# Raw weight panels in a ring of six after the mixers, with the constants' space given back

## The chip, the cores and the metric

The kernel runs on one core of one Trainium2 chip, as one launch. The metric is device time in microseconds (us) for the whole launch; a run's figure is that of the core, and the kernel's figure is the median of its runs. Traces are from the hardware profiler, one execution each.

## The reference

One decoder layer over 256 tokens of width 2048, in float32. A projection feeds two mixers (a causal multi-window pool and an RWKV-7 time mix); their outputs are concatenated and projected back; then a squared-ReLU channel mixer with 8192 hidden units, a gated per-layer embedding, and a final norm.

```python
h = rms_norm(x, attn_norm[i])
z = h @ w_in[0]
...                                      # token shift, pool mixer, RWKV-7 scan
mix = jnp.concatenate([pool_out, rwkv_out], axis=-1).astype(x.dtype)
x = x + mix @ w_out[i]

h2 = rms_norm(x, mlp_norm[i])
x = x + jnp.square(jax.nn.relu(h2 @ w_ffn_up[i])) @ w_ffn_down[i]

gate = jax.nn.sigmoid(rms_norm(x, ple_norm[i]) @ w_ple_gate[i])
x = x + gate * (p[i] @ w_ple_proj[i])
return rms_norm(x, final_norm)
```

## The kernel before

**Weights as panels.** All large weights stream from HBM once, in panels of 128 partitions x 1024 float32 (512 KB). `load_raw` (L146) takes a slot of the tag `raw` of the pool `wp`, which has three buffers, and issues one DMA from SyncE (its queue is SPq in the profile; the DMA is L148). A float32 panel is then split in two rounded parts, a high one by ScalarE (`wh`, two copies of 512 columns) and the remainder by VectorE (`wl`, one subtraction over 1024 columns). `wh` and `wl` are rings of three too. TensorE forms each product as three matmuls (high x high, low x high, high x low). The helper is `split_w` (L151; its instructions are L157 and L158); in the down projection it is `halves_of` (L1228, L1229).

**Stages.** The mixers run first, interleaved with the input projection and with half of the output projection by a hand-written order; TensorE's order is the program's up to `order.close()`. From there on a scheduler orders all engines at build time, by priority (splits and some evictions are raised by `high_priority`) and by its own model of when data and slots come free. The order on each engine, SyncE's DMA queue included, is then fixed: an instruction that waits holds up those behind it on its engine.

After that point:

- the second half of the output projection, `w_out`, 16 panels (`raw_o`), followed by the transposes `h2t`;
- `ffn_half(0)`: 64 panels of `w_ffn_up` (`raw_u`, `gemm_wide`, L1102 and L1107), then two down sweeps of 32 panels of `w_ffn_down` each (`raw_d`, `down_sweep`, L1217 to L1219), one for each half of the output columns;
- `ffn_half(1)`: the same again;
- the embedding's projection (4 panels, `raw_pp`), the gate (24 panels, `raw_gt`) and the end.

**A down sweep** goes through 16 steps `kp` of two panels (`rx`, `ry`). Most steps have 24 matmuls and two splits, `wh_d_7a`/`wl_d_7a` and `wh_d_7b`/`wl_d_7b` for step 7. The steps 1, 3, 6, 8, 11, 13 (`SEVEN`; in the last sweep 1, 3, 6, 11) take seven products for eight, 21 matmuls, at the price of four additions of panel quarters on VectorE (`td`, L1257 to L1260) and four splits: `wad` (L162, L163) and those named b, c and d. The d halves sit in the two buffers of the tag `graw`.

**Panels kept for the end.** In the last sweep (before steps 5, 8, 11, 14) and in the gate stage, `keep` (L1159 to L1164) loads a panel of the last gate quarter through the same two `graw` buffers and splits it into `gk`. Its DMA goes out on the same SyncE queue, and its split on the same ScalarE and VectorE queues.

**Memory.** `const` is a pool that lives to the end, and holds also what only the mixers read (`sbd`, `wband`, `zf`, `hsel`, `cmask` and others). `rctx` is the stack of pools that live through the mixers alone (`psr`, `rp`). It is closed behind the mixers, and the pool `fp`, for the feed-forward part, is opened in the space of `rp`.

Of the kernel before, what the change touches and what calls it, by code (L numbers as in the profile page):

```python
# [9 lines left out]
F32 = mybir.dt.float32  # L10
F32R = mybir.dt.float32r
# [5 lines left out]
T = 256  # L17
# [23 lines left out]
def trunk(  # L41
# [21 lines left out]
    const = ctx.enter_context(tc.tile_pool(name="const", bufs=1))  # L63
    wp = ctx.enter_context(tc.tile_pool(name="wp", bufs=3))
    act = ctx.enter_context(tc.tile_pool(name="act", bufs=1))
    psm = ctx.enter_context(tc.tile_pool(name="psm", bufs=4, space=PSUM))
    rctx = ctx.enter_context(ExitStack())
    psr = rctx.enter_context(tc.tile_pool(name="psr", bufs=4, space=PSUM))

    def mm_bank(name):  # L70
# [13 lines left out]
    def col(name, j):  # L84
        o = PARAM_COLS[name] + j
        return par_sb[:, o : o + 1]
# [6 lines left out]
    nc.vector.memset(eps_g, GN_EPS)  # L93
    ident = const.tile([128, 128], F32, name="ident")
    make_identity(nc, ident)
    ones = const.tile([128, 128], F32, name="ones")
    nc.vector.memset(ones, 1.0)
    jsum = const.tile([128, 128], F32, name="jsum")
    cmask = const.tile([128, 128], F32, name="cmask")
    rmask = const.tile([128, T], F32, name="rmask")  # L100
    sbd = [const.tile([128, 4, 128], F32, name=f"sbd{i}") for i in range(2)]
    nc.gpsimd.memset(cmask, 0.0)
    for r0 in (0, 64):
        nc.gpsimd.memset(cmask[r0 : r0 + 64, r0 : r0 + 64], 1.0)
    nc.gpsimd.tensor_copy(jsum, cmask)
    cen = const.tile([128, 128], F32, name="cen")
    jhead = const.tile([128, 32], F32, name="jhead")
    nc.gpsimd.memset(jhead, 0.0)
    nc.gpsimd.tensor_copy(jhead[:, 0:2], cmask[:, ::64])
    for r0 in (0, 64):  # L110
# [3 lines left out]
    nc.gpsimd.memset(rmask.rearrange("p (c t) -> p c t", t=64)[:, :, 0:1], 0.0)  # L114
    for i in range(2):
        nc.vector.memset(sbd[i], 0.0)
    edge = const.tile([128, 4, 16], F32, name="edge")
    nc.vector.memset(edge, 1.0)
    for g, win in enumerate(WINDOWS):
        for t in range(win - 1):  # L120
            nc.gpsimd.memset(edge[:, g, t : t + 1], float(win) / (t + 1))


    wband = const.tile([128, 4, 272], F32, name="wband")

    def make_bands():
        for g, win in enumerate(WINDOWS):
# [6 lines left out]
            nc.vector.tensor_tensor(w0[:, 0:128], w0[:, 0:128], ident, op=ALU.subtract)  # L134

    m0, m1 = PARAM_COLS["mu_r"], PARAM_COLS["mu_wag"] + 3
    omu = const.tile([128, m1 - m0], F32, name="omu")
    oka = const.tile([128, 8], F32, name="oka")

    def derived():  # L140
        ka0 = PARAM_COLS["k_a"]
# [1 line left out]
        nc.vector.tensor_scalar(oka, par_sb[:, ka0 : ka0 + 8], -1.0, 1.0, op0=ALU.mult, op1=ALU.add)  # L143
        nc.vector.scalar_tensor_tensor(cen, jsum, -1.0 / 64.0, ident, op0=ALU.mult, op1=ALU.add)

    def load_raw(src, n, name):  # L146
        raw = wp.tile([128, 1024], F32, tag="raw", name=f"raw_{name}")
        nc.sync.dma_start(raw[:, 0:n], src)  # L148
        return raw

# [32 lines left out]
    def gemm_cols(src, acts, name, consume, hooks=()):  # L183

        banks = [mm_bank(f"{name}_b{i}") for i in range(2)]
        nkp = src.shape[0]
        hooks = dict(hooks)
        for kp in range(nkp):
            if kp in hooks:
                hooks[kp]()  # L190
            raw = load_raw(src[kp].rearrange("p a n -> p (a n)"), 1024, f"{name}_{kp}")
            halves = split_w(raw, f"{name}_{kp}")
            for part in range(2):
                for a in range(2):
                    k = kp * 2 + a
                    ah, al = acts(k)
                    for ct in range(4):
                        o = banks[ct // 2][:, (ct % 2) * T : (ct % 2 + 1) * T]
                        w_ = halves[a][part][:, ct * 128 : (ct + 1) * 128]
                        if part:  # L200
                            nc.tensor.matmul(o, w_, ah, start=False, stop=k == 2 * nkp - 1, skip_group_check=True)
                            yield 0.12
                        else:
                            nc.tensor.matmul(o, w_, ah, start=k == 0 and ct % 2 == 0, stop=False, skip_group_check=True)
                            nc.tensor.matmul(o, w_, al, start=False, stop=False, skip_group_check=True)
                            yield 0.24
        consume(banks)

    def gemm_toks(src, acts, name, consume, kps=None, hooks=()):

        banks = [mm_bank(f"{name}_b{i}") for i in range(2)]
        kps = list(range(src.shape[0])) if kps is None else kps
        hooks = dict(hooks)
        for i, kp in enumerate(kps):
            if kp in hooks:
                hooks[kp]()
            raw = load_raw(src[kp].rearrange("p a n -> p (a n)"), 1024, f"{name}_{kp}")
            halves = split_w(raw, f"{name}_{kp}")
            for part in range(2):
                for a in range(2):  # L220
                    k = kp * 2 + a
                    a_ = acts(k)
                    ah, al = a_ if isinstance(a_, tuple) else (a_[:, 0, :], a_[:, 1, :])
                    for tt in range(2):
                        ts_ = slice(tt * 128, (tt + 1) * 128)
                        if part:
                            last = i == len(kps) - 1 and a == 1
                            nc.tensor.matmul(banks[tt], ah[:, ts_], halves[a][1], start=False, stop=last)  # L228
                            yield 0.23
                        else:  # L230
                            nc.tensor.matmul(banks[tt], ah[:, ts_], halves[a][0], start=i + a == 0, stop=False)  # L231
                            nc.tensor.matmul(banks[tt], al[:, ts_], halves[a][0], start=False, stop=False)  # L232
                            yield 0.45
        consume(banks)
# [40 lines left out]
    def run(gen):  # L275
        for _ in gen:
            pass
# [36 lines left out]
    nc.gpsimd.memset(hsel_f, 1.0)  # L314
    nc.gpsimd.affine_select(hsel_f, hsel_f, [[2048, 4], [1, 128]], ALU.is_ge, 0.0, base=0, channel_multiplier=-64)
    nc.gpsimd.affine_select(hsel_f, hsel_f, [[-2048, 4], [-1, 128]], ALU.is_ge, 0.0, base=63, channel_multiplier=64)
    hsel = const.tile([128, 4, 128], F32R, name="hsel")
    nc.gpsimd.tensor_copy(hsel, hsel_f)

    def flat(t_):  # L320
# [119 lines left out]
        nc.scalar.activation(rs1, sbank[:, 0:2], AF.Sqrt, bias=eps_n, scale=1.0 / D)  # L440
        nc.vector.reciprocal(rs1, rs1)

    zf = const.tile([128, 3, T], F32, name="zf")
    zwa, zg, zg2 = zf[:, 0], zf[:, 1], zf[0:64, 2]

    def wag_out():
# [518 lines left out]
    def pool_weights(i):  # L965
        praw = load_raw(pool_w[i].rearrange("p w k n -> p (w k n)"), 1024, f"pw{i}")
        t_ = rp.tile([128, 2, 2, 512], F32R, tag="AR", bufs=2, name=f"pws{i}")
        for wi in range(2):
            split_sb(t_[:, wi, 0], t_[:, wi, 1], praw[:, wi * 512 : (wi + 1) * 512])
        return [(t_[:, wi, 0], t_[:, wi, 1]) for wi in range(2)]  # L970
# [86 lines left out]
    def residual(banks, n):  # L1057
        for tt in range(2):
            xs = xr[tt][:, n * 512 : (n + 1) * 512]
            with tc.high_priority(30000):  # L1060
                nc.vector.tensor_tensor(xs, banks[tt], xs, op=ALU.add)
# [20 lines left out]
    fp = ctx.enter_context(tc.tile_pool(name="fp", bufs=1))  # L1082
    psw = ctx.enter_context(tc.tile_pool(name="psw", bufs=2, space=PSUM))

    def wide_bank(name):
        return psw.tile([128, 2, 512], F32, tag="wide", name=name)
# [25 lines left out]
    def transposed(name):  # L1112

        hl = fp.tile([128, 2, NK, T], F32R, tag="h2", name=name)
        h, l = hl[:, 0], hl[:, 1]

        def part(norm, n):
            for j2 in range(2 * n, 2 * n + 2):
                if j2 % 2 == 0:
                    b = wide_bank(f"{name}t")  # L1120
                for jj in range(2):
                    j = 2 * j2 + jj
                    for tt in range(2):
                        nc.tensor.transpose(
                            b[:, j2 % 2, jj * T + tt * 128 : jj * T + (tt + 1) * 128], xr[tt][:, j * 128 : (j + 1) * 128], ident
                        )
                for jj in range(2):
                    j = 2 * j2 + jj
                    src = b[:, j2 % 2, jj * T : (jj + 1) * T]
                    nc.scalar.activation(h[:, j, :], src, AF.Copy, scale=col(norm, j))  # L1130
                    nc.vector.scalar_tensor_tensor(
                        l[:, j, :], src, col(norm, j), h[:, j, :].bitcast(F32), op0=ALU.mult, op1=ALU.subtract
                    )

        return part, lambda k: hl[:, :, k, :]

    h2_part, h2 = transposed("h2")
    for n in range(4):
        run(gemm_toks(w_out[n], mix, f"o{n}", lambda banks: residual(banks, n), (6, 7, 2, 3)))
        h2_part("mlp_norm", n)  # L1140
# [331 lines left out]
```

## Time and profile before

| what | value |
|---|---|
| runs | 1190.15, 1193.17, 1196.21 us; median 1193.17 |
| profiled execution | 1191.21 us, its span 1189.5 us, granted clock 0.998 |
| TensorE matmul, weight load | 1169.6 us (98%), 974.0 us (82%) |
| VectorE, ScalarE, GpSimd | 859.2 us (72%), 702.5 us (59%), 14.0 us (1%) |
| DMA | 216.81 MB, mean 182 GB/s |

The stages after the mixers, by the busy time of the engines in them (windows chosen by hand; PE is the matmul row, DVE is VectorE, ACT is ScalarE):

| stage | window, us | PE | DVE | ACT | DMA share |
|---|---|---|---|---|---|
| output projection | 332 to 377 | 45.00 of 45 | 27.96 | 21.98 | 0.56 |
| up, first half | 377 to 556 | 178.44 of 179 | 118.12 | 97.58 | 0.58 |
| sweep 1 | 556 to 642 | 85.30 of 86 | 71.08 | 47.96 | 0.61 |
| sweep 2 | 642 to 729 | 85.89 of 87 | 73.60 | 48.31 | 0.62 |
| up, second half | 729 to 905 | 176.00 of 176 | 117.36 | 91.41 | 0.59 |
| sweep 3 | 905 to 989 | 84.00 of 84 | 70.73 | 47.73 | 0.61 |
| sweep 4 | 989 to 1080 | 88.38 of 91 | 75.56 | 55.73 | 0.71 |
| projection and gate | 1080 to 1176 | 95.87 of 96 | 52.35 | 54.62 | 0.42 |

A matmul's end is modelled in these records, so a busy PE can hide short gaps; a gap shows better in the distance of two starts. Idle time of an engine other than the one that sets the pace costs nothing by itself.

### The profile page before, as it was taken

Reading aid. Unit: us, or ns where it says so; the run is one execution under the profiler, and the core shown is the slowest. Engines: PE = TensorE matmul, PEld = TensorE weight load, DVE = VectorE, ACT = ScalarE, POOL = GpSimd, SP = SyncE. Lnnn points to the kernel's source line nnn. Section 1 sums busy time; section 2 is a strip of 40 time slices with the busy share of each in tenths; the row PEclk is TensorE's granted clock in tenths of the full one; section 3 lists DMA queues with packets and bytes.
Section 4 is the critical chain, followed back from the end, with each engine's and each line's share of the span. In section 5 each row is a group of like instructions: output and inputs, shape, how many; then the busy total and the mean of one; then the engine's idle time right before and its main releaser. Section 6 shows DMA issues by size and latency. Waiting matters only on the chain.

```text
span 1189.5 us, 17244 instructions
## 1 busy us (share of the span) xinstructions
PE 1169.6 (98%) x6428; PEld 974.0 (82%) x6428; DVE 859.2 (72%) x1156; ACT 702.5 (59%) x1302; POOL 14.0 (1%) x73
## 2 busy tenths in 40 slices
PE   9999999999999999999999999999999999999997
PEld 8787777788887888888878788888888888778886
DVE  7696996955666666667778888666678788787543
ACT  8777858676445565545555564555555555568544
POOL 2100000000000000000000000000000000000000
PEclk9999999999999999999999999999999999999999
DMA  8454443354455565566556566655555665776631
GB/s 291 158 193 143 142 142 108 118 184 154 140 180 172 181 194 187 187 193 193 181 193 197 193 207 207 192 192 190 184 193 190 200 203 188 272 245 221 206 107 71
DMA packets 60756, 216.81 MB, mean 182 GB/s; under 512 B 6784, under 2 KB 7552, under 8 KB 60288
## 3 DMA queue, kind: packets, MB, share of 16 engines
q1 hardware_dynamic: 60240, 215.12, 55.0%
q8 instruction: 50, 0.82, 0.3%
q10 hardware_dynamic: 432, 0.60, 0.1%
q14 instruction: 34, 0.28, 0.1%
HBM read 213.59 MB, written 2.10 MB: 181 GB/s over the span
## 4 chain that ended last, share of the span: by engine, by line
PE 83%; DMA 6%; DVE 5%; ACT 3%; issue 2%; SPq 0%; POOL 0%; ACTq 0%; POOLq 0%; DVEq 0%
PE u_w L1102 20%; PE u_w L1107 10%; PE d_b L1218 5%; PE d_b L1219 5%; PE d_b L1217 4%; DMA raw_d<-in_w_ffn_down_dram 4%; PE gt_b L228 2%; PE gt_b L231 2%; PE gt_b L232 2%; PE zk_b L231 1%; PE zk_b L232 1%; PE o_b L231 1%; PE o_b L232 1%; PE zv_b L228 1%; PE o_b L228 1%
## 5 line engine op out<-in xcount | busy, mean ns | idle before, releaser
L1102 PE MATMUL u_w<-h,wh_u 128*128 128x512 f32 x1024 | 321.9, 395 | 0.0
L157 ACT ACTIVATE wh_u<-raw_u 128x512 fp32r<-128x512 f32 x256 | 147.5, 623 | 164.2 <-PE u_w L1102 101.6
L158 DVE TENSOR_TENSOR wl_u<-raw_u,wh_u 128x1024 fp32r<-128x1024 f32 x128 | 156.5, 1224 | 113.3 <-ACT wh_u L157 111.7
L1107 PEld LDWEIGHTS u_w<-h,wl_u 128*128 128x128 f32 x1024 | 192.3, 188 | 45.4
L1107 PE MATMUL u_w<-h,wl_u 128*128 128x256 f32 x1024 | 201.4, 278 | 0.0
L1102 PEld LDWEIGHTS u_w<-h,wh_u 128*128 128x128 f32 x1024 | 156.0, 189 | 0.1
L158 DVE TENSOR_TENSOR wl_gt<-raw_gt,wh_gt 128x1024 fp32r<-128x1024 f32 x24 | 29.4, 1224 | 24.1 <-ACT wh_gt L157 24.0
L157 ACT ACTIVATE wh_gt<-raw_gt 128x512 fp32r<-128x512 f32 x48 | 28.0, 641 | 22.8 <-PE gt_b L232 17.2
L1257 DVE TENSOR_TENSOR td<-raw_d 128x512 f32<-128x512 f32 x22 | 15.2, 692 | 32.6 <-DMA raw_d<-in_w_ffn_down_dram 32.6
L231 PE MATMUL gt_b<-wh_gt,h 128*128 128x512 f32 x96 | 37.3, 389 | 0.0
L232 PE MATMUL gt_b<-wh_gt,h 128*128 128x512 f32 x96 | 37.3, 389 | 0.0
L162 ACT ACTIVATE wad<-raw_d 128x512 fp32r<-128x512 f32 x22 | 13.9, 632 | 36.6 <-DMA raw_d<-in_w_ffn_down_dram 36.4
L158 DVE TENSOR_TENSOR wl_o<-raw_o,wh_o 128x1024 fp32r<-128x1024 f32 x16 | 19.6, 1223 | 12.9 <-ACT wh_o L157 11.4
L157 ACT ACTIVATE wh_o<-raw_o 128x512 fp32r<-128x512 f32 x32 | 18.4, 623 | 16.3 <-issue 6.9
L157 ACT ACTIVATE wh_zp<-raw_zp 128x512 fp32r<-128x512 f32 x32 | 18.6, 623 | 15.9 <-PE zp_b L232 7.2
L158 DVE TENSOR_TENSOR wl_zk<-raw_zk,wh_zk 128x1024 fp32r<-128x1024 f32 x16 | 19.4, 1222 | 9.9 <-ACT wh_zk L157 9.9
L231 PE MATMUL zv_b<-wh_zv,hTh 128*128 128x512 f32 x64 | 26.0, 406 | 0.0
L231 PE MATMUL zk_b<-wh_zk,hTh 128*128 128x512 f32 x64 | 25.2, 394 | 0.7 <-ACT wh_zk L157 0.7
L231 PE MATMUL zp_b<-wh_zp,hTh 128*128 128x512 f32 x64 | 25.7, 401 | 0.0
L228 PE MATMUL gt_b<-wl_gt,h 128*128 128x512 f32 x96 | 25.7, 389 | 0.0
L157 ACT ACTIVATE wh_zk<-raw_zk 128x512 fp32r<-128x512 f32 x32 | 18.4, 624 | 11.9 <-DMA raw_zk<-in_w_in_dram 5.7
L231 PE MATMUL zr_b<-wh_zr,hTh 128*128 128x512 f32 x64 | 25.4, 397 | 0.0
(809 smaller groups left out, 2966.1 us busy)
## 6 DMA issues: line engine op xcount, KB each, us to landing
raw_u<-in_w_ffn_up_dram SPq DMA_DIRECT2D x128, 512.0 KB, 3.5
raw_d<-in_w_ffn_down_dram SPq DMA_DIRECT2D x128, 512.0 KB, 4.2
raw_gt<-in_w_ple_gate_dram SPq DMA_DIRECT2D x24, 512.0 KB, 3.5
raw_zk<-in_w_in_dram SPq DMA_DIRECT2D x16, 512.0 KB, 3.8
raw_zr<-in_w_in_dram SPq DMA_DIRECT2D x16, 512.0 KB, 3.3
raw_zv<-in_w_in_dram SPq DMA_DIRECT2D x16, 512.0 KB, 3.4
raw_zp<-in_w_in_dram SPq DMA_DIRECT2D x16, 512.0 KB, 3.3
raw_o<-in_w_out_dram SPq DMA_DIRECT2D x16, 512.0 KB, 3.6
```

Source lines behind the costliest of these rows:

```text
L157: nc.scalar.activation(wh[:, a * 512 : (a + 1) * 512], raw[:, a * 512 : (a + 1) * 512], AF.Copy)
L158: nc.vector.tensor_tensor(wl, raw, wh.bitcast(F32), op=ALU.subtract)
L162: nc.scalar.activation(h_ap, src_ap, AF.Copy)
L228: nc.tensor.matmul(banks[tt], ah[:, ts_], halves[a][1], start=False, stop=last)
L231: nc.tensor.matmul(banks[tt], ah[:, ts_], halves[a][0], start=i + a == 0, stop=False)
L232: nc.tensor.matmul(banks[tt], al[:, ts_], halves[a][0], start=False, stop=False)
L1102: nc.tensor.matmul(bank[:, ct, :].rearrange("p (s t) -> p s t", s=2), wh[:, cs[ct]], hl, start=k == 0, stop=False, skip_group_check=True,)
L1107: nc.tensor.matmul(bank[:, ct, 0:T], wl[:, cs[ct]], hl[:, 0, :], start=False, stop=k == 15, skip_group_check=True)
L1217: nc.tensor.matmul(banks[n], ah, wh, start=first, stop=False)
L1218: nc.tensor.matmul(banks[n], ah, wl, start=False, stop=False)
L1219: nc.tensor.matmul(banks[n], al, wh, start=False, stop=last)
L1257: nc.vector.tensor_tensor(t1, rx[:, 512:1024], rx[:, 0:512], op=ALU.subtract)
```

## The change

A new pool `mixc` is opened on the stack `rctx`, and twelve groups of tiles that only the mixers read move from `const` to it: `ones`, `jsum`, `cmask`, `rmask`, two `sbd`, `cen`, `jhead`, `edge`, `wband`, `omu`, `oka`, `hsel`, `zf`. By their shapes they are 17,164 bytes on each partition. They are released with `rctx`, so `fp` can reach down into their place.

`load_raw` gets a second ring. From `deep.append("w_out")` on it counts its loads; the first four take slots of `wp`'s tag `raw` as before, the next three slots of a new tag `raw2` with three buffers in `fp` (3 x 4,096 bytes on each partition), the next three `raw` again, and so on in turns of three. A slot is then taken again after six loads and not after three. This holds for 301 loads: 16 of `w_out`, 128 of up, 128 of down, 1 of `pT`, 4 of the projection, 24 of the gate. The rings `wh`, `wl`, `graw`, `wa` and the tile of `td` keep their sizes. No instruction is added or taken away.

```diff
     rctx = ctx.enter_context(ExitStack())
+    mixc = rctx.enter_context(tc.tile_pool(name="mixc", bufs=1))
     psr = rctx.enter_context(tc.tile_pool(name="psr", bufs=4, space=PSUM))
...
-    ones = const.tile([128, 128], F32, name="ones")
+    ones = mixc.tile([128, 128], F32, name="ones")
...
-    sbd = [const.tile([128, 4, 128], F32, name=f"sbd{i}") for i in range(2)]
+    sbd = [mixc.tile([128, 4, 128], F32, name=f"sbd{i}") for i in range(2)]
...
+    deep = []
+
     def load_raw(src, n, name):
-        raw = wp.tile([128, 1024], F32, tag="raw", name=f"raw_{name}")
+        own = False
+        if deep:
+            deep.append(name)
+            own = len(deep) > 5 and len(deep) % 6 < 3
+        if own:
+            raw = fp.tile([128, 1024], F32, tag="raw2", bufs=3, name=f"raw_{name}")
+        else:
+            raw = wp.tile([128, 1024], F32, tag="raw", name=f"raw_{name}")
         nc.sync.dma_start(raw[:, 0:n], src)
         return raw
...
-    zf = const.tile([128, 3, T], F32, name="zf")
+    zf = mixc.tile([128, 3, T], F32, name="zf")
...
     h2_part, h2 = transposed("h2")
+    deep.append("w_out")
     for n in range(4):
         run(gemm_toks(w_out[n], mix, f"o{n}", lambda banks: residual(banks, n), (6, 7, 2, 3)))
```

More of the change, by code (lines that the diff above doesn't have):

```diff
@@ L95, in trunk @@
     make_identity(nc, ident)
-    ones = const.tile([128, 128], F32, name="ones")
+    ones = mixc.tile([128, 128], F32, name="ones")
     nc.vector.memset(ones, 1.0)
-    jsum = const.tile([128, 128], F32, name="jsum")
-    cmask = const.tile([128, 128], F32, name="cmask")
-    rmask = const.tile([128, T], F32, name="rmask")
-    sbd = [const.tile([128, 4, 128], F32, name=f"sbd{i}") for i in range(2)]
+    jsum = mixc.tile([128, 128], F32, name="jsum")
+    cmask = mixc.tile([128, 128], F32, name="cmask")
+    rmask = mixc.tile([128, T], F32, name="rmask")
+    sbd = [mixc.tile([128, 4, 128], F32, name=f"sbd{i}") for i in range(2)]
     nc.gpsimd.memset(cmask, 0.0)
@@ L105, in trunk @@
     nc.gpsimd.tensor_copy(jsum, cmask)
-    cen = const.tile([128, 128], F32, name="cen")
-    jhead = const.tile([128, 32], F32, name="jhead")
+    cen = mixc.tile([128, 128], F32, name="cen")
+    jhead = mixc.tile([128, 32], F32, name="jhead")
     nc.gpsimd.memset(jhead, 0.0)
@@ L116, in trunk @@
         nc.vector.memset(sbd[i], 0.0)
-    edge = const.tile([128, 4, 16], F32, name="edge")
+    edge = mixc.tile([128, 4, 16], F32, name="edge")
     nc.vector.memset(edge, 1.0)
@@ L121, in trunk @@
             nc.gpsimd.memset(edge[:, g, t : t + 1], float(win) / (t + 1))
-    wband = const.tile([128, 4, 272], F32, name="wband")
+    wband = mixc.tile([128, 4, 272], F32, name="wband")
     def make_bands():
@@ L136, in trunk @@
     m0, m1 = PARAM_COLS["mu_r"], PARAM_COLS["mu_wag"] + 3
-    omu = const.tile([128, m1 - m0], F32, name="omu")
-    oka = const.tile([128, 8], F32, name="oka")
+    omu = mixc.tile([128, m1 - m0], F32, name="omu")
+    oka = mixc.tile([128, 8], F32, name="oka")
     def derived():
@@ L316, in trunk @@
     nc.gpsimd.affine_select(hsel_f, hsel_f, [[-2048, 4], [-1, 128]], ALU.is_ge, 0.0, base=63, channel_multiplier=64)
-    hsel = const.tile([128, 4, 128], F32R, name="hsel")
+    hsel = mixc.tile([128, 4, 128], F32R, name="hsel")
     nc.gpsimd.tensor_copy(hsel, hsel_f)
```

## The prediction, made before any run of the changed kernel

> **What bounds the kernel now.** I read the page first, then the windows by stage (the table above), then the waits of TensorE behind the mixers, and last the chain of work at the longest of those waits. From the page:
>
> ```profile
> span 1189.5 us, 17244 instructions
> PE 1169.6 (98%) x6428; PEld 974.0 (82%) x6428; DVE 859.2 (72%) x1156; ACT 702.5 (59%) x1302; POOL 14.0 (1%) x73
> ```
>
> TensorE sets the pace nearly everywhere. So a deeper ring of panels can win only what TensorE loses for want of a panel, and only in the stages behind the mixers. The waits of TensorE from 332 us on (total, times, longest) are the whole purse:
>
> ```profile
> PE d_b L1218 <- DVE wl_d_8b L1229: 0.9, 1, 0.9
> PE h3t L1124 <- DVE x L1237: 0.7, 1, 0.7
> PE d_w L1218 <- DVE wl_d_6d L1229: 0.7, 1, 0.7
> PE d_b L1218 <- DVE wl_d_7b L1229: 0.6, 2, 0.4
> PE h2t L1124 <- DVE x L1061: 0.6, 1, 0.6
> PE d_b L1218 <- DVE wl_d_6b L1229: 0.5, 1, 0.5
> PE d_b L1218 <- DVE wl_d_12b L1229: 0.3, 1, 0.3
> PE h3t L1124 <- DVE ud L1276: 0.3, 1, 0.3
> PE d_w L1218 <- DVE wl_d_6c L1229: 0.2, 1, 0.2
> PE d_b L1217 <- DVE x L1237: 0.2, 1, 0.2
> ```
>
> Eleven waits, 5.0 us in total; seven of them, 3.2 us, are waits for the low part of a down panel, and none lies in an up stage. These idle times are short by a fixed amount, as one of them shows in the timeline of TensorE (start, duration, instruction, idle before it):
>
> ```profile
> 596.42 0.39 PE L1219 MATMUL d_b<-wh_d_7a,y 128*128 128x512 f32 x1
> 596.65 0.39 PE L1217 MATMUL d_b<-wh_d_7b,y 128*128 128x512 f32 x1
> 597.41 0.50 PE L1218 MATMUL d_b<-wl_d_7b,y 128*128 128x512 f32 x1 [0.37 <-DVE wl_d_7b L1229]
> ```
>
> Starts are 0.23 us apart where nothing waits, while a matmul is drawn 0.39 us long, so each wait costs 0.39 - 0.23 = 0.16 us more than the idle time shown: here 0.76 - 0.23 = 0.53 us for an idle time of 0.37.
>
> What stands behind that wait is in the chain of work of the same stretch:
>
> ```profile
> 589.29 0.70 DVE td L1260
> 590.04 4.28 DMA raw_d<-in_w_ffn_down_dram
> 594.42 0.06 ACT wad L162
> 594.96 1.15 ACT wh_d_7b L1228 x2
> 596.13 1.24 DVE wl_d_7b L1229
> ```
>
> The panel of step 8 (split as `wad`) could not be asked for until VectorE's last addition of step 6 gave a slot of the ring of three back, at 589.99. It then took 4.28 us, and on ScalarE its split stood ahead of `wh_d_7b`, for which the data were there. That is the pattern the change is aimed at: slot late, load late, engine queue held, TensorE short by half a microsecond.
>
> **The change part by part.**
>
> *More slots (the gain).* Each load behind the mixers may go out three panels earlier. The pace of TensorE is in a row of the chain (four matmuls of the same shape on one panel, nothing waiting), and the landings are in the table of DMA issues (count, KB, median us from issue to landing):
>
> ```profile
> 332.30 0.91 PE o_b L228 x4
> ```
>
> ```profile
> raw_d<-in_w_ffn_down_dram SPq DMA_DIRECT2D x128, 512.0 KB, 4.2
> graw<-in_w_ple_gate_dram SPq DMA_DIRECT2D x8, 512.0 KB, 5.0
> ```
>
> Four matmuls take 0.91 us; a plain step has 24 for its two panels, 24 x 0.91 / 4 = 5.46 us, or 2.7 us a panel. Three panels are then 8.2 us, more than these landings. So I take away whole the waits for `wl_d_7b` (two), `wl_d_6b`, `wl_d_6c`, `wl_d_12b` and `wl_d_8b`: 0.6 + 0.5 + 0.2 + 0.3 + 0.9 = 2.5 us of idle time in six waits, and 6 x 0.16 = 1.0 more. That makes 3.5 us. The wait for `wl_d_8b` has another history, as the chain of the last sweep shows together with the one for `wl_d_6d`:
>
> ```profile
> 1015.54 7.08 DMA graw<-in_w_ple_gate_dram
> 1022.64 1.16 ACT gk L1163 x2
> 1025.09 1.24 DVE wl_d_6d L1229
> 1026.37 0.50 PE d_w L1218
> 1027.86 5.98 DMA raw_d<-in_w_ffn_down_dram
> 1033.95 1.16 ACT wh_d_8b L1228 x2
> 1036.42 0.50 PE d_b L1218
> ```
>
> The first half is a kept panel of the gate: its DMA, its split, and only then `wl_d_6d`, because both want the two `graw` buffers. The ring of raw panels has no part in that; `graw` stays at two. Only the 7.08 us could get shorter, towards the 5.0 of the median row, by 2.1 us, as less urgent panels crowd it. That would remove the wait whole (0.7 + 0.16 = 0.86 us); if the crowding stays, nothing goes. I take half, 0.4 us. In the second half SyncE's queue was held, as its own waits in the last sweep show:
>
> ```profile
> SPq L1159 <- DVE wl_d_6d L1229: 4.2, 1, 4.2
> ```
>
> A second kept panel's DMA waited 4.2 us for its buffer with the raw panel of step 8 behind it, and with three slots more that panel has been asked for before.
>
> *In the up stages and the gate* nothing is won. ScalarE and VectorE wait there for something else than panels (the waits of the whole run: total, times, longest):
>
> ```profile
> ACT wh_u L157 <- PE u_w L1102: 101.6, 79, 1.6
> ACT wad L162 <- DMA raw_d<-in_w_ffn_down_dram: 36.4, 19, 3.2
> DVE td L1257 <- DMA raw_d<-in_w_ffn_down_dram: 32.6, 20, 3.6
> ```
>
> The first row says that the split of an up panel waits for TensorE to give back a `wh` buffer, a ring that stays at three. The other two are the 69 us that the down sweeps wait for panels on engines beside the path; most of that can vanish and move the end by no more than the 3.9 us above.
>
> *The constants' space.* The first loads into `raw2` and the first write of `h2` must wait until the last reader of what lay there is done. By the timeline of TensorE the last matmuls that read the mixers' tiles start at:
>
> ```profile
> 316.57 0.28 PE L172 MATMUL pm<-d,pws 128*128 128x256 f32 x1
> ```
>
> The constants are read for the last time in the steps before that in TensorE's fixed order. So the space is free at about 317 us. The first panel that goes there is the fifth of `w_out`. The row of the chain above ends TensorE's work on the first at 333.2 us, and the fourth ends three panels later, at 333.2 + 8.2 = 341.4 us. So 24 us cover a landing of 4.2 and a split of 1.15 + 1.24. Cost: nothing; without that cover, the landing and the split, 6.6 us once. The tiles' new addresses change no instruction of the mixers; nothing, on either side.
>
> *Instructions and queues.* No DMA, split or matmul is added. The 301 loads are the same, in the same queue. But the order that the scheduler fixes behind the mixers is drawn anew, because panels come free earlier in its model. What stays the same is the ring of `wh` and `wl`, which holds the splits to three halves ahead, so I price the new order at nothing and keep 2 us to both sides for it: about the two longest waits above, 0.9 + 0.7 with 0.16 each.
>
> *Sum.* 3.5 + 0.4 = 3.9 us off the profiled execution's 1191.2 us gives 1187.3. That execution lay 2.0 us under the median of the runs, 1193.17; against the median the forecast is 1189.3 us.
>
> *A rule on the other side of the sum.* Busy matmul rows may hide more than the waits show, so I worked the sum out a second way, by weight loads in the windows (PE, PEld, DVE, ACT, POOL busy with counts, clock, DMA share, GB/s):
>
> ```profile
> 556.00:642.00 86.00, 85.30 (x377) 69.60 (x375) 71.08 (x80) 47.96 (x85) 0.00 (x0) 1.00 0.61 194
> 642.00:729.00 87.00, 85.89 (x377) 69.55 (x376) 73.60 (x84) 48.31 (x85) 0.00 (x0) 1.00 0.62 200
> 905.00:989.00 84.00, 84.00 (x374) 69.45 (x373) 70.73 (x80) 47.73 (x84) 0.00 (x0) 1.00 0.61 198
> 989.00:1080.00 91.00, 88.38 (x391) 70.84 (x390) 75.56 (x86) 55.73 (x102) 0.00 (x0) 1.00 0.71 245
> ```
>
> What is late next, once the loads are early, is VectorE: it is busy 71.1 of 86 and 73.6 of 87 us in sweeps 1 and 2, the first two rows. Sweep 3, with 70.7 of 84, has no wait at all, and it loads weights 69.45 / 84 = 0.827 of its time. Were the others as dense, they would take 69.60 / 0.827 = 84.2, 84.1 and 85.7 us, 1.8 + 2.9 + 5.3 = 10 us less. That is the top of what can be won: 1193.2 - 10 = 1183.2 us. The listed waits explain 6.8 of the 10 us (5.0 + 11 x 0.16). The Trainium skill (Perfetto Trace Analysis, Identifying the Most-Contended Engine) has the rule behind it: matmul busy time is no good measure of the distance to the roof, and the busy share of weight loads is one. The trace agrees in part, since TensorE's row shows 84.00 of 84 us and 85.30 of 86 where weight loads show 0.827 and 0.809.
>
> **The rivals.**
>
> *Nothing is won (0.20).* The loads come early, but the splits still come late, since `wh` and `wl` stay at three and VectorE is 83 and 85% busy in sweeps 1 and 2, or the scheduler lets additions of a later step go ahead of the urgent split as it did with `wad`. For it: the waits name VectorE's subtraction and not the DMA. Against it: sweep 3 has the same work on VectorE (70.73 us in 84) and no wait. Time: 1193.2 less at most 1 us, so 1192.5.
>
> *All gaps close (0.12).* The hand-overs to `h2t` and `h3t` go as well, since VectorE has caught up when they come. For it: sweep 3. Against it: those waits are for additions of finished sums, and the last sweep's own kept panels remain. Time: 1193.2 - 10 = 1183.2 at the best, 1186.4 if only the waits listed go.
>
> *Slower: the kept panels end up behind the raw ones (0.18).* SyncE's queue goes in order. With six slots the scheduler may place up to three more raw loads ahead of a `graw` load, and each stands there until its slot is free on the chip. Three loads are 8.2 us, as above. The split `gk` sits in the queues of ScalarE and VectorE at a place fixed at build time, so both stand still for the kept panel. The `wh` and `wl` parts that TensorE has in hand then last it two panels' halves, 5.4 us; the mechanism decides from two extra loads on, and with three it costs 8.2 - 5.4 = 2.7 us for each kept panel. With the four of the last sweep that is 11 us, less the 2.4 us that the first two sweeps still win (their five waits, 1.6 + 5 x 0.16): 1201.8 us; with all eight, some 1212. For it: the 4.2 us above, and what ScalarE already loses ahead of `gk`:
>
> ```profile
> ACT gk L1163 <- DMA graw<-in_w_ple_gate_dram: 6.5, 6, 3.8
> ```
>
> Against it: the raw loads ahead would mostly have a free slot, and then wait for nothing. The Trainium skill (DMA: Bandwidth & Descriptors, Queues, rings and completion order) adds that the loads which one engine issues share one row of rings and are consumed in ring order, so that a kept panel behind more panels also lands later. No row here shows that order; the trace agrees so far that `graw` took 7.08 us for a median of 5.0 in the sweep with the highest DMA share, 0.71.
>
> *The change does not do what it says.* By the counting of `deep`, loads 5 to 7, 11 to 13 and so on go to `raw2`, so a slot is taken again after six loads; I give this no chance of its own.
>
> **How the numbers follow.** Forecast 0.50, nothing won 0.20, all gaps 0.12, slower 0.18. A median of this kernel can tell about 0.5%, or 6.0 us, from no change: below 1187.2 is faster, above 1199.1 slower. The forecast's own range is 1186.5 to 1192. Faster: 0.08 from the third case and 0.07 from the low end of the first, 0.15. Slower: 0.17 from the last case and 0.01 of the rest. The range leaves out the low end of the third case (0.06) and the upper part of the last (0.12): 1184.5 to 1202.
>
> **What would show it.** In the profile after: the rows of ScalarE and VectorE waiting for `raw_d` fall from 69 us to under 20; SyncE's waits name older splits; TensorE's waits for `wl_d_7b`, `wl_d_6b`, `wl_d_12b` and `wl_d_8b` are gone, and that for `wl_d_6d` remains or halves; sweeps 1 and 2 end 1.0 and 1.4 us shorter, the last some 1.5; up stages and mixers keep their lengths. The forecast is wrong if the mixers' part before 332 us changes its length, if TensorE shows waits at the hand-overs to the up stages, or if `gk` makes ScalarE idle for longer than the 6.5 us before a kept panel that the whole run has now.

## The result and the profile after

The changed kernel takes 1187.2 us in the median (1185.86 to 1190.06, 13 runs) against 1193.04 us for the kernel before on the same chip (1189.83 to 1196.21, 13 runs). The ratio of the means is 0.9955, with a 95% interval of 0.9943 to 0.9967: 5.4 us less, between 3.9 and 6.8 (the medians lie 5.8 us apart). The profiled execution took 1189.19 us, its span 1187.5.

The page of the changed kernel (first line, engines, chain by engine), and below it the chain line of the page before:

```profile
span 1187.5 us, 17266 instructions
PE 1169.3 (98%) x6428; PEld 976.9 (82%) x6428; DVE 857.7 (72%) x1156; ACT 704.8 (59%) x1302; POOL 14.1 (1%) x73
PE 93%; ACT 2%; DVE 2%; DMA 2%; issue 0%; POOL 0%; SPq 0%; DVEq 0%; ACTq 0%; POOLq 0%
```

```profile
PE 83%; DMA 6%; DVE 5%; ACT 3%; issue 2%; SPq 0%; POOL 0%; ACTq 0%; POOLq 0%; DVEq 0%
```

No engine has more or less to do. What moved is the chain that ended last: DMA, VectorE and ScalarE stand in it with 6% in place of 14%.

The waits of TensorE behind the mixers in the changed kernel (total, times, longest; lines are 10 or 11 higher than before):

```profile
PE d_w L1229 <- DVE wl_d_6d L1240: 1.1, 1, 1.1
PE d_b L1228 <- DVE x L1248: 0.7, 2, 0.4
PE h3t L1134 <- DVE x L1248: 0.7, 2, 0.5
PE h2t L1134 <- DVE x L1071: 0.6, 1, 0.6
```

Six of the seven waits for a down panel are gone. The one for `wl_d_6d` is left, and it is longer. ScalarE's and VectorE's largest waits for down panels over the whole run:

```profile
DVE td L1268 <- DMA raw_d<-in_w_ffn_down_dram: 5.1, 6, 1.5
ACT wad L172 <- DMA raw_d<-in_w_ffn_down_dram: 4.4, 2, 2.2
```

They were 69 us and are 9.5. Stages are compared best by the start of their first matmul, because a window cut by hand is met by another stage when something ahead of it moves. The four sweeps of the changed kernel, each from its first matmul to the first of what follows (PE, PEld, DVE, ACT, POOL busy with counts, clock, DMA share, GB/s):

```profile
560.23:643.65 83.42, 83.14 (x369) 68.59 (x367) 66.79 (x76) 47.92 (x84) 0.00 (x0) 1.00 0.60 197
643.65:727.12 83.47, 83.47 (x366) 68.56 (x367) 71.48 (x81) 46.96 (x82) 0.00 (x0) 1.00 0.60 205
905.46:988.97 83.51, 83.13 (x368) 68.59 (x367) 67.36 (x76) 48.07 (x84) 0.00 (x0) 1.00 0.60 194
988.97:1078.56 89.59, 87.83 (x392) 71.43 (x393) 74.71 (x85) 55.64 (x102) 0.00 (x0) 1.00 0.73 253
```

Cut in the same way, the kernel before has 369, 366, 369 and 394 matmuls in 84.91, 85.09, 83.04 and 91.19 us: the same work in more time. How the pattern of the prediction dissolves is to be seen around step 7 of sweep 1, first on ScalarE, then on VectorE:

```profile
592.78 0.62 ACT L172 ACTIVATE wad<-raw_d 128x512 fp32r<-128x512 f32 x1
593.76 1.16 ACT L1239 ACTIVATE wh_d_7b<-raw_d 128x512 fp32r<-128x512 f32 x2 [0.36 <-PE d_b L1230]
```

```profile
595.18 1.22 DVE L1240 TENSOR_TENSOR wl_d_7b<-raw_d,wh_d_7b 128x1024 fp32r<-128x1024 f32 x1
```

The split `wad` of step 8 still stands ahead of `wh_d_7b`, but its panel is there and it holds nothing up. `wh_d_7b` now waits for TensorE to free a `wh` buffer. At this place that ring is the next thing that ScalarE waits for.

By their first matmuls, the two up stages take 179.20 us (179.21 after) and 178.36 us (178.34). The sweeps, in all profiles of this study:

| profile | sweep 1 | 2 | 3 | 4 | sum |
|---|---|---|---|---|---|
| before | 84.91 | 85.09 | 83.04 | 91.19 | 344.2 |
| before, again (b2, b3) | 84.31, 83.90 | 84.79, 85.86 | 83.03, 83.61 | 92.76, 92.41 | 344.9, 345.8 |
| constants moved only (e1) | 83.27 | 85.50 | 83.59 | 90.48 | 342.8 |
| six slots except in the sweeps (e3) | 82.97 | 85.28 | 84.02 | 92.84 | 345.1 |
| changed kernel | 83.42 | 83.47 | 83.51 | 89.59 | 340.0 |
| changed kernel, again (a2) | 83.27 | 83.51 | 83.76 | 91.87 | 342.4 |
| six slots in the sweeps alone (e2) | 83.00 | 83.32 | 83.39 | 89.67 | 339.4 |
| four slots (e4) | 83.02 | 82.96 | 83.25 | 90.33 | 339.6 |
| six slots, three `graw` (e5) | 83.62 | 83.47 | 82.97 | 89.56 | 339.6 |
| three slots, three `graw` (e6) | 85.12 | 85.02 | 83.17 | 96.10 | 349.4 |
| six slots, kept panels later (e7) | 83.54 | 83.47 | 82.97 | 88.12 | 338.1 |
| program order, three slots (m3) | 101.19 | 102.98 | 100.94 | 125.17 | 430.3 |
| program order, six slots (m6) | 91.95 | 92.04 | 91.72 | 116.71 | 392.4 |

### The profile page after: what moved, and what is told of

Same layout as the page of the kernel before. It is cut to its first block, busy times and chain, and to the rows that moved or that the text cites. A ratio compares the mean times of both kernels' runs of the same rounds, so it can differ in the third digit from the quotient of the medians.

```text
span 1187.5 us, 17266 instructions
## 1 busy us (share of the span) xinstructions
PE 1169.3 (98%) x6428; PEld 976.9 (82%) x6428; DVE 857.7 (72%) x1156; ACT 704.8 (59%) x1302; POOL 14.1 (1%) x73
## 4 chain that ended last, share of the span: by engine, by line
PE 93%; ACT 2%; DVE 2%; DMA 2%; issue 0%; POOL 0%; SPq 0%; DVEq 0%; ACTq 0%; POOLq 0%
PE u_w L1112 20%; PE u_w L1117 10%; PE d_b L1228 7%; PE d_b L1229 7%; PE d_b L1230 7%; PE gt_b L242 2%; PE gt_b L238 2%; PE gt_b L241 2%; PE d_w L1229 2%; PE d_w L1230 2%; PE d_w L1228 2%; PE zk_b L241 1%; PE zk_b L242 1%; PE zk_b L238 1%; PE o_b L241 1%; PE o_b L242 1%
## 5 line engine op out<-in xcount | busy, mean ns | idle before, releaser
L242 PE MATMUL zk_b<-wh_zk,hTl 128*128 128x512 f32 x64 | 25.5, 399 | 0.0
L168 DVE TENSOR_TENSOR wl_zv<-raw_zv,wh_zv 128x1024 fp32r<-128x1024 f32 x16 | 19.4, 1220 | 8.2 <-ACT wh_zv L167 7.3
```

Source lines behind the costliest of these rows:

```text
L168: nc.vector.tensor_tensor(wl, raw, wh.bitcast(F32), op=ALU.subtract)
```

## The experiments

The theory (S) is that the gain is the down panels being asked for earlier, and nothing else. Its rivals are the new place of the tiles (P), gains at the hand-overs between stages (H), and the order of the engines that the scheduler drew anew (O). For O there was cause: against the kernel before, some 25 of the 4,230 rows of TensorE's order stand at another place (equal matmuls in a row are one row), some 50 on ScalarE and over 150 on VectorE.

**Only the constants moved (e1).**

```diff
     h2_part, h2 = transposed("h2")
-    deep.append("w_out")
```

> The constants are moved to the pool that is released, and the ring of raw panels stays at three; the order of instructions on every engine is that of the kernel before. Theory S (slots: down panels asked for earlier are the whole gain): 0, within 1.5 us of the kernel before, with all its waits of TensorE in the sweeps. Rival P (placement: the new addresses of the mixers' tiles or of the feed-forward tiles change something): a part of the 5 us, seen as a shorter or longer mixers' part.

The edit is made to the changed kernel, as are all that follow. 1191.8 us, ratio 0.9994 (0.9982 to 1.0007). The order on TensorE, VectorE and ScalarE is that of the kernel before, row by row, and the waits of TensorE are back; three of them:

```profile
PE d_b L1228 <- DVE wl_d_8b L1239: 1.0, 1, 1.0
PE d_b L1228 <- DVE wl_d_6b L1239: 0.4, 1, 0.4
PE d_b L1228 <- DVE wl_d_7b L1239: 0.4, 1, 0.4
```

The addresses do nothing that shows (between 2.1 us less and 0.8 us more); P as the cause of the gain is out.

**Six slots for the sweeps alone (e2), and for everything else (e3).**

```diff
-        if deep:
+        if deep and name[0] == "d":      # e2; in e3: name[0] != "d"
```

> Six slots for the panels of the four down sweeps alone; the output projection, up, embedding projection and gate keep three. Theory S: the whole gain, 4.5 to 5.5 us, sweeps 1, 2 and 4 each about 1.5 us shorter. Rival H (the hand-overs between stages gain too, from panels of the next stage being there early): 1 to 2 us less than the whole.

> The complement: six slots for the output projection, up, embedding projection and gate, three in the down sweeps. Theory S: 0, within 1.5 us of the kernel before, the waits for wl_d_7b, wl_d_12b, wl_d_6b and wl_d_8b back. Rival H: 1 to 2 us faster than before.

e2: 1186.9 us, ratio 0.995 (0.9935 to 0.9964). e3: 1192.27 us, ratio 0.9999 (0.9986 to 1.0013). The longest waits of TensorE in the sweeps, e2 first:

```profile
PE d_w L1229 <- DVE wl_d_6d L1240: 1.8, 1, 1.8
```

```profile
PE h3t L1134 <- DVE x L1248: 1.8, 2, 1.6
PE d_b L1229 <- DVE wl_d_8b L1240: 1.3, 1, 1.3
PE d_b L1229 <- DVE wl_d_6b L1240: 0.8, 1, 0.8
PE d_b L1229 <- DVE wl_d_7b L1240: 0.7, 2, 0.4
```

The sweeps have the whole gain, and all other stages none that shows, though in e3 their panels were asked for earlier too (the first up panel at 357.3 us and not at 364.7). H is out as the main cause; e3's interval leaves it at most 1.7 us.

**Four slots (e4).**

```diff
-            own = len(deep) > 5 and len(deep) % 6 < 3
+            own = len(deep) > 5 and len(deep) % 4 == 0
...
-            raw = fp.tile([128, 1024], F32, tag="raw2", bufs=3, name=f"raw_{name}")
+            raw = fp.tile([128, 1024], F32, tag="raw2", bufs=1, name=f"raw_{name}")
```

> Four slots instead of six, in all stages behind the mixers: each load can go out one panel (2.7 us) earlier, not three (8.2 us). The stalls of the kernel before are 0.4 to 1.05 us each, so by theory S 2.7 us are enough for nearly all of them: 80% or more of the gain, 4 to 5 us. Rival O (the gain is luck of the order that the scheduler draws, which is another one here): anything between 2 us slower and 5 us faster, with waits of TensorE at other places.

1187.24 us, ratio 0.9951 (0.9936 to 0.9965): the whole gain, with one slot more in place of three and with another order (some 20 rows of TensorE's order stand elsewhere than in the changed kernel). Its two longest waits:

```profile
PE h3t L1134 <- DVE x L1248: 2.1, 1, 2.1
PE d_w L1229 <- DVE wl_d_6d L1240: 0.9, 1, 0.9
```

For stalls of 0.2 to 0.9 us, one panel of lead, 2.7 us, is enough; the other two slots bring nothing that shows.

**The same order with three and with six slots (m3, m6).** To part S from O, the sweeps of both kernels were held to the order of the program text on TensorE, VectorE, ScalarE and SyncE.

```diff
-    def down_sweep(hf, pair, ys, sboxes, hooks=(), between=None, seven=SEVEN):
+    def down_sweep(*args):
+        with tc.manual_schedule(engines={mybir.EngineType.PE, mybir.EngineType.DVE, mybir.EngineType.Activation, mybir.EngineType.SP}):
+            sweep(*args)
+
+    def sweep(hf, pair, ys, sboxes, hooks=(), between=None, seven=SEVEN):
...
-    deep.append("w_out")                 # m3 alone
```

> Three slots, and in the four down sweeps TensorE, VectorE, ScalarE and SyncE keep the order of the program text instead of the scheduler's. The additions of finished sums then stand in VectorE's queue ahead of the next splits, so it should be slower than the kernel before, by 10 to 40 us. It is the base for the kernel with six slots in the same order.

> Six slots, with the same order of instructions on all engines in the sweeps as the kernel with three slots and the program's order. Theory S (early loads by themselves): 3 to 6 us faster than that one, with fewer waits of ScalarE and VectorE for panels. Rival O (the gain came from the order that the scheduler drew anew, not from the slots on the chip): within 1 us of it.

m3: 1279.15 us, ratio 1.0723 (1.0701 to 1.0745). m6: 1239.89 us, ratio 1.0399 (1.0379 to 1.0419). Both expected sizes were far too small, 10 to 40 us for the order and 3 to 6 for the slots; the measured ones are 87 and 39 us. The direction is S's. In sweeps 1 and 2 TensorE waits in m3 (the five longest groups), and then in m6 (all), as follows:

```profile
PE d_b L1232 <- DVE wl_d_14a L1243: 10.5, 2, 5.2
PE d_w L1232 <- DVE wl_d_6c L1243: 3.2, 2, 1.9
PE d_w L1232 <- DVE wl_d_3c L1243: 3.1, 2, 1.6
PE d_w L1232 <- DVE wl_d_13c L1243: 3.0, 2, 1.5
PE d_b L1231 <- ACT wh_d_14a L1242: 2.6, 2, 1.3
```

```profile
PE d_b L1233 <- DVE wl_d_14a L1244: 10.5, 2, 5.2
PE d_b L1232 <- ACT wh_d_14a L1243: 2.6, 2, 1.3
```

What the order costs in these two sweeps, the additions behind step 13 ahead of the splits of step 14, is the same in both, 13.1 us. The waits for the splits c and for 6b are in m3 alone, and with six slots all of them go. In the sweeps the two orders differ by a few splits of hidden units at the start and by some transposes, kept panels and products of the next stage at the end. So early loads work by themselves in one order, the program's, where they are worth 39 us; in the scheduler's order the change is worth 5.4. The scheduler's order of the kernel before thus seems to have hidden most of what three slots cost. The changed kernel's own order was not run with three slots, so what part of the 5.4 us is due to the order alone isn't shown; that e4 has the same gain with another order speaks against a large one.

**The wait that is left (e5, e6, e7).** In sweep 4 of the changed kernel ScalarE and then VectorE do this ahead of the wait at 1024 us:

```profile
1020.94 1.15 ACT L1174 ACTIVATE gk<-graw 128x512 fp32r<-128x512 f32 x2 [1.47 <-DMA graw<-in_w_ple_gate_dram]
```

```profile
1022.13 1.23 DVE L1175 TENSOR_TENSOR gk<-graw,gk 128x1024 fp32r<-128x1024 f32 x1 [1.40 <-ACT gk L1174]
1023.27 1.22 DVE L1240 TENSOR_TENSOR wl_d_7a<-raw_d,wh_d_7a 128x1024 fp32r<-128x1024 f32 x1
1024.41 1.22 DVE L1240 TENSOR_TENSOR wl_d_6d<-td,wh_d_6d 128x1024 fp32r<-128x1024 f32 x1
```

The kept panel is waited for, split, and even the split of step 7 now stands ahead of `wl_d_6d`, which followed `gk` directly before (1023.83 and 1025.09 us). Three edits aimed at that: a third `graw` buffer with six slots (e5) and with three (e6), and the kept panels asked for later (e7).

```diff
# e5 and e6 (halves_of likewise; e6 also without the line deep.append)
-        raw = fp.tile([128, 1024], F32, tag="graw", bufs=2, name=f"graw{kp}")
+        raw = fp.tile([128, 1024], F32, tag="graw", bufs=3, name=f"graw{kp}")
# e7
-            down_sweep(hf, 1, ys, sboxes, {5: keep, 8: keep, 11: keep, 14: keep}, ...)
+            down_sweep(hf, 1, ys, sboxes, {7: keep, 9: keep, 12: keep, 14: keep}, ...)
```

> The changed kernel with a third graw buffer, so that a kept panel and the two halves d of a step have a buffer each. Theory S with the remaining wait for wl_d_6d put down to the two graw buffers: that wait, 1.1 us idle and 1.3 us by the starts, goes, 1.0 to 1.5 us faster than the changed kernel, some 6.5 us faster than before. Rival: the kept panels go out earlier and crowd the raw panels or take VectorE's time from the urgent splits; no gain over the changed kernel, or up to 1 us lost.

> Three raw slots, as before, with a third graw buffer: in the last sweep SyncE's queue is no longer held for a graw buffer. If the wait for wl_d_8b came from SyncE standing 4.2 us with the raw panel of step 8 behind it, both waits of the last sweep go: 1.5 to 2 us faster than before, sweeps 1 and 2 as before. If that wait came from the three raw slots alone, only the wait for wl_d_6d goes: 0.5 to 1.0 us.

> The changed kernel with the four kept panels of the last sweep asked for before steps 7, 9, 12 and 14 instead of 5, 8, 11 and 14, so that none stands between a step with halves d (6 and 11) and its graw buffers. If the remaining wait for wl_d_6d is the kept panel's doing, the last sweep gets 1 to 1.5 us shorter (about 88.3 us) and the kernel as much faster than the changed one. Rival: the wait moves to another step or to the transposes h3t, as it did with a third graw buffer; the last sweep stays within 0.5 us of 89.6.

e5: 1186.08 us, ratio 0.9953 (0.9936 to 0.9971). e6: 1193.6 us, ratio 1.0011 (0.9997 to 1.0025). e7: 1185.8 us, ratio 0.9952 (0.9934 to 0.9971). Waits of TensorE in sweep 4 of each, the longest first, in that order:

```profile
PE h3t L1134 <- DVE ud L1287: 0.9, 1, 0.9
PE d_b L1229 <- DVE wl_d_9a L1240: 0.8, 1, 0.8
```

```profile
PE h3t L1134 <- DVE ud L1286: 3.8, 1, 3.8
PE d_b L1228 <- DVE wl_d_9a L1239: 0.5, 1, 0.5
```

```profile
PE h3t L1134 <- DVE x L1248: 0.7, 1, 0.7
```

With a third buffer the wait for `wl_d_6d` goes and as much comes back at other places; e5 gains nothing that shows over the changed kernel, which was the rival of its expectation. In e6 the wait for `wl_d_8b` goes without any raw slot, so SyncE's standing still for a `graw` buffer had a part in it. Yet nothing is won of the 1.5 to 2 us that were expected for this case: in the profile the transposes wait 3.8 us and sweep 4 takes 96.1 us. That execution, 1196.39 us, is one of the two slowest of twelve (the fastest took 1189.07), so it shows what can happen and not the usual size. The chain of work ahead of that wait (`SPq` is SyncE's queue):

```profile
1051.20 0.70 DVE td L1270
1051.96 0.33 SPq L158
1052.34 6.34 DMA graw<-in_w_ple_gate_dram
1058.70 0.04 ACT gk L1173
1059.23 1.14 ACT wh_d_13a L1238 x2
1060.40 1.23 DVE wl_d_13a L1239
1062.28 0.66 PE h3t L1134 x4
```

Here a kept panel went out behind two raw loads that had to wait for VectorE's additions to free a slot; it landed at 1058.7, and the split of step 13, in ScalarE's queue behind `gk`, came late. This is the slower rival of the prediction, in a kernel with three slots. With the kept panels later the last sweep takes 88.1 us, as expected, but the stage behind it 0.4 us more (12.88 for 12.44). By the profile e7 is the best of all, but that execution was the fastest of its six; by the times it can't be told from the changed kernel.

**Second and third profiles (b2, b3 of the kernel before, a2 of the changed one).**

> The kernel before once more, for a second look at its waits. If its waits for panels vary from one execution to the next, the four sweeps differ by 1 us or more in their sum from the 344.2 us of the first profile, with waits at other steps; if they are fixed by the order of the engines, the sum is within 0.3 us.

> The same kernel before, a third look, with the same expectations. Theory V (the first profile was one of the better executions, and the median one loses a microsecond or two more in the sweeps): the sum of the four sweeps is 344 to 347 us in both looks.

> The changed kernel once more. Its loads have 8 us of cover, so its four sweeps should vary less than those of the kernel before: their sum within 0.5 us of the 340.0 us of its first profile.

Single runs of 1192.26, 1191.99 and 1188.41 us. The kernel before, in four profiles with the same order of instructions (e1 is one of them), takes 342.8 to 345.8 us for its sweeps, so these vary by 3 us from one execution to the next; the idle time of their waits for down panels varies from 3.1 to 5.1 us. (b2's sum, 344.9 us, fits neither side of its expectation; b3's, 345.8, says that they vary.) The changed kernel's second profile missed the expectation: 342.4 us for 340.0. Most of the distance is in the granted clock of TensorE, the third number from the end, in sweep 4 behind a wait of 1.9 us:

```profile
1020.00:1025.00 5.00, 3.14 (x12) 2.23 (x11) 5.00 (x5) 2.87 (x6) 0.00 (x0) 0.86 0.66 248
1025.00:1030.00 5.00, 5.00 (x19) 4.01 (x18) 0.54 (x1) 0.88 (x2) 0.00 (x0) 0.79 0.65 202
```

That is 5 x 0.14 + 5 x 0.21 = 1.75 us of lost clock; without it the sum is 340.7, still 0.2 us outside the expectation. The wait itself is 0.8 us longer than in the first profile (1.86 for 1.11). So the changed kernel's sweeps vary as well, and that they vary less isn't shown.

## Why the prediction was right, and where its sizes were off

It forecast 1189.3 us, a gain of 3.9; measured are 5.4 us (3.9 to 6.8). The median, 1187.2 us, lies inside the range, near its fast end, and the gain is clear of the noise though under the 0.5% named there.

- *The purse.* That only what TensorE loses can be won, and only in the sweeps: e3 (nothing) and e2 (all) show it. The 69 us of waits on ScalarE and VectorE fell to 9.5 us and brought about 5.
- *The six waits taken away whole, 3.5 us.* They are gone. Taking the means of the profiles (before, b2, b3, e1 against changed, a2 without its 1.75 us, e2), sweep 1 is 84.1 - 83.2 = 0.9 us shorter (forecast 1.0), sweep 2 85.3 - 83.4 = 1.9 (forecast 1.4), sweep 3 0.2 longer (forecast 0), sweep 4 91.7 - 89.8 = 1.9 shorter (forecast 1.5), and the stage behind it 0.4: 4.9 us in all.
- *Mis-sized: what a wait costs beside its idle time.* The prediction added 0.16 us to each. But the matmul behind a wait is itself drawn longer, 0.50 us, and the next one follows 0.34 us after it and not 0.23. Behind the wait that the prediction shows, which ended at 597.41, the next matmul is this:

```profile
597.75 0.40 PE L1219 MATMUL d_b<-wh_d_7b,y 128*128 128x512 f32 x1
```

  All seven waits for down panels in the first profile have these 0.33 or 0.34 us. So a wait costs some 0.16 + 0.11 = 0.27 us beside its idle time, and the six make 0.7 us more: 4.2 in place of 3.5.
- *One execution, and what is left open.* Without the wait for `wl_d_6d`, the idle time of waits for down panels is 2.5 us in the first profile (six waits), 2.6 in b2 (four), 4.5 in b3 (eight) and 2.3 in e1 (six). At 0.27 us each that is 4.6 us in the mean, an estimate; three of the four profiles agree, and the first, with 344.2 us for its sweeps, isn't one of the better ones there (mean 344.4). The longer wait for `wl_d_6d` takes about 1 us back, and shorter waits at the transposes and gaps too short to be listed must give a little more than that; these aren't told apart, nor is the distance from 4.9 to 5.4 us, which is inside the interval.
- *Wrong: half of the wait for `wl_d_6d` goes, 0.4 us.* It grew, from 0.7 us of idle time to 1.1, and 1.8 and 1.9 in e2 and a2. The step that failed is "if the crowding stays, nothing goes" as the worse end, and with it the new order at nothing. The crowding did ease: this kept panel took 5.6 us from issue to landing (1015.31 to 1020.92) in place of 7.08, and 6.3 and 6.4 in e2 and a2. But the kept panel was still waited for, and the new order put `wl_d_7a` ahead of the urgent split; it holds VectorE from 1023.27 to 1024.41, 1.14 us by the starts, as much as the whole wait of 1.11. Shorter waits for the transposes `h3t` (1.0 us before, 0.7 after) paid for part of it.
- *The constants' space and the new order at nothing.* The first is shown by e1. The second held within its 2 us on this order and on that of e4, but m3 and m6 show how much an order can weigh: 87 us with three slots, and some 53 with six (48 against the kernel before, and the 5.4 that six slots win there).
- *The rival by weight loads, 10 us.* In windows that begin and end with the stage, sweeps 1, 2 and 4 load weights 80.4, 80.2 and 77.9% of their time before and 82.2, 82.1 and 79.7% after; sweep 3 has 82.6 and 82.1%. So sweeps 1 and 2 were brought nearly to the density of sweep 3, and sweep 4 less than half the way. The rule of the Trainium skill on weight loads (Perfetto Trace Analysis, Identifying the Most-Contended Engine) pointed the right way; the listed waits, 6.8 us, were nearer to the size. That all gaps close did not come true, for the waits at the transposes and for `wl_d_6d` are still there.
- *The slower rival, kept panels behind raw ones.* It did not come with the change: ScalarE's waits ahead of `gk` fell from 6.5 to 5.1 us. Why isn't shown; raw loads still wait for slots in front of kept panels, in sweep 4 up to 6.1 us until the split `wl_d_7a` frees one. The mechanism can happen, though: e6 has it with three slots, and its sweep 4 is 4.4 us longer than the mean before, some 1.7 us of it by the clock, which is 0.50 for 3.4 us behind the wait of 3.8 us.
- *The mixers* were to keep their length, and in the profile of the changed kernel the output projection begins 2.6 us later. That is no effect of the change: a2, of the same kernel, begins it at 329.8 us, and before it was 330.3. In the changed kernel's first profile the granted clock fell between 35 and 50 us, before first, after second, and then the part of it at half the clock:

```profile
35.00:50.00 15.00, 14.12 (x74) 11.30 (x74) 9.42 (x23) 12.24 (x24) 4.24 (x15) 1.00 0.45 155
```

```profile
35.00:50.00 15.00, 13.91 (x65) 11.14 (x64) 8.77 (x21) 10.70 (x20) 4.23 (x15) 0.89 0.47 152
38.11:41.52 3.41, 3.41 (x12) 2.67 (x11) 2.73 (x10) 2.16 (x3) 2.51 (x9) 0.50 0.16 62
```

  At 0.89, 15 us lose 1.65 of the 2.6 us. The same fall is in e3 and m6 (0.89 over the same stretch), and these two begin the output projection late too, at 331.9 and 331.8 us; the eleven profiles without it begin it between 329.6 and 331.1. The late start is also why the profile's span fell by only 2.0 us.

## What to carry to other kernels

When an engine is 98% busy, price a deeper buffer by that engine's own waits, measured from start to start until the pace is back, and not by the waits of the engines that feed it; then take several profiles, because such waits vary from one execution to the next. One buffer more was enough here, since each wait was shorter than the time in which one panel is used up. Where loads of two kinds share an in-order queue and a small pool of buffers, freeing one of them moves the wait to the next user, so look at who waits next before adding the buffer.

## What the hardware showed that was not expected

A wait of TensorE can be followed by a loss beside its length, because the granted clock is lower behind it. In m3, around 698 us, TensorE's timeline and then the window of the lower clock:

```profile
698.54 0.79 PE L1232 MATMUL d_w<-wl_d_6c,S 128*128 128x512 f32 x1 [1.95 <-DVE wl_d_6c L1243]
699.56 0.63 PE L1231 MATMUL d_w<-wh_d_6c,S 128*128 128x512 f32 x1
699.98 0.63 PE L1232 MATMUL d_w<-wl_d_6c,S 128*128 128x512 f32 x1
```

```profile
698.58:702.00 3.42, 3.42 (x8) 2.74 (x9) 2.69 (x3) 1.63 (x3) 0.00 (x0) 0.50 0.75 256
```

Behind 1.95 us of idle time the starts are 0.42 us apart and not 0.23, and the clock is 0.50 for 3.4 us, which loses 1.7 us. The same follows two waits of 1.94 us in m3 (ended at 960.6 and 1056.6 us) and the one of 1.86 us in a2. The length alone does not decide: a wait of 1.61 us in m3, 1.82 in e2 and 2.07 in e4 had no such effect, while the fall at 38.11 us above came behind a wait of only 1.08 us. What decides isn't shown here. The Trainium skill (TensorE: Matmul & The Clock Gate, Why this matters for your kernels) warns of gaps above about 3 us; here waits of 1.86 to 1.95 us were followed by the fall in four places, and the measurement decides. The kernel before has no wait of that length in its first profile, so this played no part in the prediction's sum. It has a part in the 39 us between m3 and m6: 61 us of m3's sweeps and 48 us of m6's have the half clock, which makes at most 7 us of the 39.
